# Convolution gates of three channel pairs as seven products of quarters, with weight sums made in DRAM

## The chip, the cores and the metric

The kernel runs on one core of a Trainium2 chip. The metric is the device time of one execution in microseconds (us), the median of several runs. The core has a matrix engine (PE, with its weight loads shown apart as PEld), a vector engine (DVE), a scalar engine (ACT), GpSimd (POOL) and a sync engine (SP), which here only issues transfers. Each has its own queue of instructions and waits for the others by semaphores.

## The reference

Two layers over 512 tokens of width D = 1024. Layer 0 mixes tokens with a forgetting attention, layer 1 with a short gated convolution. After each mixer come a squared-ReLU MLP (1024 to 4096 to 1024) and a gated per-layer embedding (PLE); every sub-layer stands between two RMS norms and is added to the residual. The change is in layer 1's mixer:

```python
def short_conv(h, w_in, conv_w, w_out):
    proj = h @ w_in                      # w_in: 1024 x 3072
    b_gate = proj[..., :D]
    c_gate = proj[..., D:2 * D]
    u = proj[..., 2 * D:]
    z = c_gate * u
    zc = causal_depthwise_conv(z, conv_w)   # 3 taps
    return (b_gate * zc) @ w_out

def sq_relu_mlp(h, w_up, w_down):
    return jnp.square(jax.nn.relu(h @ w_up)) @ w_down
```

Everything is float32.

## The kernel before

**One matmul is three.** PE works on float32 values rounded to its own format, fp32r. `mm3` (L224) splits each operand into a rounded part (hi) and the remainder (lo) and issues three matmuls: hi by hi (L226), hi by lo or lo by hi (L227, L228). `split` (L232) makes the parts: ACT rounds (L234), DVE subtracts (L235).

**Weights are streamed.** All weight tiles of the kernel stand in one list in the order of use. `fetch` (L117) brings the next, 256 KB as 128 rows of 512 values, into one of 14 raw buffers by a transfer on SP (L123); `prepare` (L137) splits it into the tiles `wh` and `wl`, eight tiles ahead of their use (`SOON`, L34). They live in a pool of 70 pages of 128x512. Results gather in 8 PSUM banks of 128x512.

**The MLP.** Hidden channels are worked in eight groups of 512 (`mlp`, L728). `up` makes a group's activations. `down` (L774) multiplies groups 0 to 6 by seven products of quarters in Winograd's form of Strassen's scheme: tokens by halves of the group on the one side, halves of the group by halves of the output on the other (PRODUCTS, L49; order of the products in STEPS, L53: 1, 2, 4, 5, 6, 7, 3). The weight side needs the sums T1 to T4, which `derive` (L125) makes on POOL from raw tiles; their lo parts, `wl<-T`, are also split on POOL. The activations' sums s are made on POOL as well (`quarters`, L757, sums at L760). `acc` banks gather the seven results over the groups.

**The convolution.** `conv` (L675) goes over four pairs of channel blocks, i0 = 0, 2, 4, 6; a block is 128 channels. `gates` (L690) makes c and u of a block, each by 8 k tiles x 3 = 24 matmuls, copies c to an SBUF page (ACT, L695) and multiplies (DVE, L696). `finish` (L700) makes b in the same way, applies the three taps (ACT L704, DVE L707), multiplies by b (L711) and splits the result for the output projection. Pair 0 is done in two halves of 256 tokens, so that it can begin before the last tokens of the layer before are ready; the other three pairs take 512 tokens at once. Its input `hT` is the normed and transposed residual, written as hi and lo by `pre_norm` (L288) in layer 0's PLE. Pairs read 12 weight tiles each (`wci`).

**Order.** A scheduler orders each engine's instructions by its own estimates of when each can run, from the order in which the program issues them; only few places set the order by hand. A pool's buffer is reused in program order.

Of the kernel before, what the change touches and what calls it, by code (L numbers as in the profile page):

```python
# [8 lines left out]
F32 = mybir.dt.float32  # L9
F32R = mybir.dt.float32r  # L10
AF = mybir.ActivationFunctionType
ALU = mybir.AluOpType
# [3 lines left out]
P = 128  # L16
D = 1024
S = 512
# [3 lines left out]
KT = D // P  # L22
# [30 lines left out]
STEPS = (1, 2, 4, 5, 6, 7, 3)  # L53


class Pair:


# [5 lines left out]


@with_exitstack
def trunk(ctx: ExitStack, tc, g4T, x, xT, pT, g, g0T, wv, wqk, bf, wo, wci, cw, wco, wup, wdn, wpp, wpg, out):
# [8 lines left out]
    dram = pool("dram", 1, space=DRAM)  # L76
# [40 lines left out]
    def fetch(upto):  # L117
        while len(fetched) < min(upto, len(loads)):
            n = len(fetched)
            raw = raws.tile([P, S], F32, tag="raw", name=f"raw{n}")  # L120
            fetched.append(raw)
            src = loads[n]
            nc.sync.dma_start(raw[:, : src.shape[-1]], src)  # L123

    def derive(l, gr):  # L125
        at = derived.pop((l, gr))
# [35 lines left out]
    def wide(*key, soon=SOON):  # L162

        prepare(where[key] + 1 + soon)
        return ready[key]

    def narrow(*key, k, c, soon=SOON):

        c += k % 2 * 256
        return wide(*key, k // 2, soon=soon).at(lambda u: u[:, c : c + P])  # L170

    for l in range(2):
        if l == 0:
            for c, (_, width) in enumerate(V_CHUNKS):
                for k in range(KT * width // 512 if width < 272 else KT):
                    plan(("v", c, k), wv[c][k])
            for i in range(KT):
                for j in range(4):
                    plan(("qk", i, j), wqk[i, j])
            for k in range(KT):  # L180
                for n in range(2):
                    plan(("o", n, k), wo[n, k])
        else:
            for i in range(0, KT, 2):
                for s, key in enumerate((("cu", i), ("b", i), ("cu", i + 1))):
                    for j in range(4):
                        plan((*key, j), wci[3 * (i // 2) + s, j])
# [100 lines left out]
    def pre_norm(t, xs, gB, hT, name):  # L288

        r = stats(t, xs, name)  # L290
        hs = [scaled(t, n, xs, r, gB, name) for n in range(2)]

        def turn():
            for n in range(2):
                keep(t, n, turned(t, n, hs[n], name), hT)

        put_off(t, turn)

# [373 lines left out]
            pass  # L672
        return oT[0], banks_o

    def conv(hT):  # L675
        taps = consts.tile([P, KT, 3], F32, tag="taps", name="taps")
        nc.sync.dma_start(taps, cw)
        ys = []

        def project(key, s, name, lo, hi):  # L680
            need(*range(lo // P, hi // P))
            ps = bank(name)
            for k in range(KT):
                mm3(
                    ps[:, : hi - lo], narrow(*key, k=k, c=s * P),
                    hT.at(lambda h: h[:, k, lo:hi]), k == 0, k == KT - 1,
                )
            return ps

        def gates(i, z, lo, hi):  # L690
            n = hi - lo
            c = project(("cu", i), 0, f"c{i}_{lo}", lo, hi)
            u = project(("cu", i), 1, f"u{i}_{lo}", lo, hi)
            cs = page(f"cs{i}_{lo}")
            nc.scalar.copy(cs[:, :n], c[:, :n])  # L695
            nc.vector.tensor_tensor(  # L696
                out=z[:, lo:hi], in0=u[:, :n], in1=cs[:, :n], op=ALU.mult
            )

        def finish(i, z, y, lo, hi):  # L700
            n = hi - lo
            b = project(("b", i - i % 2), i % 2, f"b{i}_{lo}", lo, hi)
            a = page(f"za{i}_{lo}")
            nc.scalar.mul(a[:, :n], z[:, lo:hi], taps[:, i, 2:3])  # L704
            for w in (1, 0):
                c = max(2 - w - lo, 0)
                nc.vector.scalar_tensor_tensor(  # L707
                    out=a[:, c:n], in0=z[:, lo + c + w - 2 : hi + w - 2],
                    scalar=taps[:, i, w : w + 1], in1=a[:, c:n], op0=ALU.mult, op1=ALU.add,
                )  # L710
            nc.vector.tensor_tensor(out=a[:, :n], in0=b[:, :n], in1=a[:, :n], op=ALU.mult)  # L711
            split(y.hi[:, lo:hi], y.lo[:, lo:hi], a[:, :n])

        for i0 in range(0, KT, 2):
# [12 lines left out]

    def mlp(l, hT, xs, then, late):  # L728
# [28 lines left out]
        def quarters(gr, f, q, s, A):  # L757

            L, R = slice(0, S // 2), slice(S // 2, S)
            sums = lambda out, a, b, op: nc.gpsimd.tensor_tensor(out=out, in0=a, in1=b, op=op)  # L760
# [56 lines left out]

        total, hs, gB = combine(), [], []
# [83 lines left out]
    hT = turned_x  # L902
# [4 lines left out]
    kind = "o"  # L907
    xs = [load_x("xb", t) for t in range(NB)]
    for l in range(2):
        if l == 1:  # L910
            lhs, kind, opened = conv(hT), "co", {}
        g1, g2 = gain(l, 1), gain(l, 2)
        hT = turned_x
        mixer_out(
# [28 lines left out]
        if l == 0:  # L943
            g0 = gain(1, 0)
            hT = turned_x
            then = lambda t: pre_norm(t, xs[t], g0, hT, "n0b")
# [11 lines left out]
def layout(x, p, norm_g, w_attn_in, b_forget, w_attn_out, w_conv_in, conv_w, w_conv_out,  # L958
# [26 lines left out]
    ci = np.stack([c[:, :, 0], u[:, :, 0], b[:, :, 0], b[:, :, 1], c[:, :, 1], u[:, :, 1]], axis=2)  # L985
    got["wci"] = tiles(ci.reshape(D, 3 * D), 2, 256)
# [26 lines left out]
```

## Time and profile before

| | |
|---|---|
| runs | 1230.38, 1230.71, 1231.73 us; median 1230.71 |
| the profiled execution | 1231.44 us |
| its span in the profile | 1229.7 us |
| PE busy | 1213.8 us, 99%, 5976 matmuls, granted clock 0.998 |
| DVE, ACT, POOL busy | 857.4, 673.5 and 642.2 us |
| transfers | 145.54 MB, mean 118 GB/s |

The trace shows one execution; start times count from the start of its span. In a row of groups the columns are line, engine, operation, out<-in, shapes, count, then busy us and mean ns of one, then idle time before and what ended it. In a row of the timeline they are start, length, engine, line, operation, out<-in, shapes and count of instructions taken together. Busy times of neighbouring matmuls overlap by some, so the pace of matmuls is read from windows or from starts.

### The profile page before, as it was taken

What the parts mean: (1) busy time and instruction counts of PE and PEld (TensorE: products, weight loads), DVE (VectorE), ACT (ScalarE), POOL (GpSimd) and SP (SyncE); (2) the same over time, 40 slices, a digit from 0 to 9 for tenths busy, and PEclk for the clock granted to TensorE, in tenths of its full rate; (3) what the DMA queues carried; (4) which work ended last, traced back from release to release, by engine and by line L of the source; (5) the groups of instructions that cost most, each with busy time, mean ns of one, the idle gap of its engine ahead of it and who ended that gap; (6) DMA issues with size and microseconds to landing.
All of it is one profiled execution on the core that took longest, in us unless ns stands there. A gap on an engine that the chain in (4) does not pass through costs nothing.

```text
span 1229.7 us, 17957 instructions
## 1 busy us (share of the span) xinstructions
PE 1213.8 (99%) x5976; PEld 1025.7 (83%) x5976; DVE 857.4 (70%) x1306; ACT 673.5 (55%) x1382; POOL 642.2 (52%) x650
## 2 busy tenths in 40 slices
PE   9999999999999999999999999999999999999997
PEld 8888887888888888888889888889888888888885
DVE  5668888585778766879757444556767787669952
ACT  6567888558634563456744322335756345645641
POOL 2058676057877877775310000027867878678220
PEclk9999999999999999999999999999999999999999
DMA  9564542623244223437323233432422443236401
GB/s 293 189 183 120 138 127 63 206 98 98 72 137 138 88 69 119 137 95 266 103 69 104 69 103 93 149 119 70 138 69 76 130 137 101 63 111 191 134 19 51
DMA packets 84173, 145.54 MB, mean 118 GB/s; under 512 B 10032, under 2 KB 17248, under 8 KB 84080
## 3 DMA queue, kind: packets, MB, share of 16 engines
q1 hardware_dynamic: 83648, 143.87, 38.0%
q8 instruction: 47, 0.77, 0.3%
q10 hardware_dynamic: 432, 0.53, 0.1%
q14 instruction: 46, 0.38, 0.1%
HBM read 137.99 MB, written 6.37 MB: 117 GB/s over the span
## 4 chain that ended last, share of the span: by engine, by line
PE 91%; DVE 3%; ACT 2%; DMA 2%; issue 1%; POOL 1%; SPq 0%; DVEq 0%; POOLq 0%; ACTq 0%
PE up L228 9%; PE up L226 9%; PE up L227 9%; PE dn L228 8%; PE dn L227 8%; PE dn L226 8%; PE pg L228 2%; PE pg L226 2%; PE pg L227 2%; PE qk L226 2%; PE qk L227 2%; PE qk L228 2%; PE v L227 1%; PE sc L495 1%; PE v L228 1%; PE v L226 1%
## 5 line engine op out<-in xcount | busy, mean ns | idle before, releaser
L235 DVE TENSOR_TENSOR wl<-raw,wh 128x512 fp32r<-128x512 f32 (+1 forms) x372 | 352.3, 993 | 24.6 <-ACT wh L234 16.7
L227 PE MATMUL up<-hTl,wh 128*128 128x512 f32 (+1 forms) x576 | 210.4, 366 | 0.5 <-DVE hTl L235 0.5
L228 PE MATMUL up<-hTh,wl 128*128 128x512 f32 (+1 forms) x576 | 209.7, 366 | 0.0
L226 PE MATMUL up<-hTh,wh 128*128 128x512 f32 (+1 forms) x576 | 209.6, 366 | 0.0
L234 ACT CAST wh<-raw 128x512 fp32r<-128x512 f32 (+1 forms) x372 | 202.9, 618 | 3.4 <-DMA raw<-in_wv 3.1
L235 POOL TENSOR_TENSOR wl<-T,wh 128x512 fp32r<-128x512 f32 x112 | 155.9, 1421 | 32.6 <-ACT wh L234 31.3
L746 ACT ACTIVATE r<-up 128x512 f32<-128x512 f32 (+1 forms) x72 | 39.3, 546 | 203.2 <-PE up L228 203.2
L792 DVE TENSOR_TENSOR acc<-dn,acc 128x512 f32<-128x512 f32 x168 | 107.9, 679 | 26.5 <-PE dn L228 26.5
L227 PEld LDWEIGHTS up<-hTl,wh 128*128 128x128 f32 x576 | 108.7, 189 | 18.2 <-DVE hTl L235 0.7
L228 PEld LDWEIGHTS up<-hTh,wl 128*128 128x128 f32 x576 | 108.7, 189 | 17.3
L226 PEld LDWEIGHTS up<-hTh,wh 128*128 128x128 f32 x576 | 108.4, 189 | 17.5
L135 POOL TENSOR_TENSOR T<-raw,raw 128x512 f32<-128x512 f32 x56 | 87.9, 1580 | 50.5 <-DMA raw<-in_wdn 36.9
L135 POOL TENSOR_TENSOR T<-raw,T 128x512 f32<-128x512 f32 x56 | 90.4, 1614 | 2.2
L256 POOL TENSOR_SCALAR cor_r_v<-cos,cos 128x1 f32<-128x1 f32 x4 | 1.8, 439 | 158.9 <-ACT junk L264 158.8
L234 ACT CAST wh<-T 128x512 fp32r<-128x512 f32 x112 | 61.4, 616 | 7.0 <-POOL T L135 7.0
L235 DVE TENSOR_TENSOR A12l<-q,A12h 128x512 fp32r<-128x512 f32 x28 | 24.5, 876 | 50.9 <-ACT A12h L234 50.9
L235 DVE TENSOR_TENSOR A11l<-q,A11h 128x256 fp32r<-128x256 f32 x28 | 25.4, 906 | 40.6 <-ACT A11h L234 40.6
L799 POOL TENSOR_TENSOR acc<-acc,acc 128x512 f32<-128x512 f32 x28 | 47.1, 1713 | 10.0 <-DVE acc L792 10.0
L226 PE MATMUL qk<-hTh,wh 128*128 128x512 f32 x128 | 51.0, 398 | 0.0
L226 PE MATMUL pg<-wh,hTh 128*128 128x512 f32 x128 | 50.5, 395 | 0.0
L228 PE MATMUL qk<-hTh,wl 128*128 128x512 f32 x128 | 50.5, 394 | 0.0
L227 PE MATMUL qk<-hTl,wh 128*128 128x512 f32 x128 | 50.2, 393 | 0.0
(246 smaller groups left out, 3160.4 us busy)
## 6 DMA issues: line engine op xcount, KB each, us to landing
raw<-in_wup SPq DMA_DIRECT2D x128, 256.0 KB, 2.9
raw<-in_wdn SPq DMA_DIRECT2D x128, 256.0 KB, 2.8
raw<-in_wci SPq DMA_DIRECT2D x48, 256.0 KB, 3.1
raw<-in_wqk SPq DMA_DIRECT2D x32, 256.0 KB, 5.9
raw<-in_wpg SPq DMA_DIRECT2D x32, 256.0 KB, 3.5
g<-in_g SPq DMA_DIRECT2D x18, 256.0 KB, 6.4
prl<-neg_c SPq DMA_DIRECT2D x16, 256.0 KB, 6.9
raw<-in_wo SPq DMA_DIRECT2D x16, 256.0 KB, 2.8
```

What stands on the lines that cost most here:

```text
L135: nc.gpsimd.tensor_tensor(out=B[name, p], in0=B[a, p], in1=B[b, p], op=ALU.subtract)
L226: nc.tensor.matmul(ps, a.hi, b.hi, start=start, stop=False)
L227: nc.tensor.matmul(ps, a.hi, b.lo, start=False, stop=False)
L228: nc.tensor.matmul(ps, a.lo, b.hi, start=False, stop=stop)
L234: nc.scalar.copy(hi, src)
L235: eng.tensor_tensor(out=lo, in0=src, in1=hi.bitcast(F32), op=ALU.subtract)
L256: nc.gpsimd.tensor_scalar(out=v, in0=parts[0], scalar1=parts[1], scalar2=EPS, op0=ALU.add, op1=ALU.add)
L495: nc.tensor.matmul(ps[:, :nm], at[:, b * P : n], to[:, :nm], start=s == 0, stop=s == 1)
L746: nc.scalar.activation(r[:, :n], ps[:, :n], AF.Relu)
L792: nc.vector.tensor_tensor(out=a, in0=banks[s], in1=a, op=ALU.add)
L799: nc.gpsimd.tensor_tensor(out=a, in0=a, in1=acc[i, s][:, :S], op=ALU.add)
```

## The change

For the pairs i0 = 2, 4, 6 the c and u projections are one product of a 512x1024 by a 1024x512 matrix (tokens by k, and k by the four blocks c and u of both blocks of the pair), cut into quarters: token halves by k halves, and k halves by two channel blocks. `sevenths` makes the seven products, in the order 1, 6, 7, 5, 2, 4, 3 (PARTS), each two column halves x 4 k tiles x 3 matmuls of 256 columns. DVE combines them (U, V, W, c11, c12, c21, c22, all 128x512; ACT copies the first product to `cp`), and z comes from four half products. b stays as it was, and pair 0 too.

The token side needs four sums (s1 to s4). For them eight fp32 copies of the transposed tokens (`plain`) are made by ACT out of PSUM when `hT` is written, and `token_sums`, called once within pair 0, makes and splits the sums.

The weight side needs t1 to t4 for each of the three pairs. They are made in DRAM while layer 0's MLP runs: `sum_weights(gr)` is called after `up` of group gr. In group 0 SP copies a quarter into each of t1 and t3 (six transfers of 512 KB), in group 1 GpSimd adds another quarter with accumulating transfers (six), in group 2 t1 is copied to t2 (three), in group 3 b22 is added (three), in group 4 t2 is copied to t4 and in group 5 b21 is added. Copies are issued behind the group's last raw fetch, accumulates behind its last quarter sum. Each pair then streams 14 tiles for the products and 4 for b in place of 12.

```diff
+SUMS_W = {"t1": ("b11", "b12"), "t3": ("b12", "b22"), "t2": ("t1", "b22"), "t4": ("t2", "b21")}
+SUM_STEPS = (
+    (("t1", "copy"), ("t3", "copy")), (("t1", "add"), ("t3", "add")), (("t2", "copy"),),
+    (("t2", "add"),), (("t4", "copy"),), (("t4", "add"),), (),
+)
+PARTS = (
+    (1, "a11", "b11"), (6, "s2", "t2"), (7, "s3", "t3"), (5, "s1", "t1"),
+    (2, "a12", "b21"), (4, "a22", "t4"), (3, "s4", "b22"),
+)
...
-            nc.sync.dma_start(raw[:, : src.shape[-1]], src)
+            behind["copy"] = nc.sync.dma_start(raw[:, : src.shape[-1]], src)
...
+    def sum_weights(step):
+
+        of = lambda n, i: sums_w[n][i] if n in sums_w else wcs[QUARTERS.index(n), i]
+        for name, kind in SUM_STEPS[step]:
+            a, b = SUMS_W[name]
+            with tc.issue_after(behind[kind].ins):
+                for i in range(3):
+                    if kind == "copy":
+                        nc.sync.dma_start(sums_w[name][i], of(a, i))
+                    else:
+                        nc.gpsimd.dma_start(
+                            sums_w[name][i], of(b, i), accum_op=ALU.add, max_dma_last_dim=2048
+                        )
...
+        def token_sums():
...
+                for name, a, b, op in (
+                    ("s3", p[0, 0], p[1, 0], ALU.subtract), ("s1", p[1, 1], p[1, 0], ALU.subtract),
+                    ("s2", p[0, 0], "s1", ALU.add), ("s4", "s2", p[0, 1], ALU.subtract),
+                ):
...
+                    nc.vector.tensor_tensor(out=t[:, :S], in0=a, in1=b, op=op)
...
+        def sevenths(i0):
...
+            for i, a, b in PARTS:
+                ps = bank(f"sq{i}_{i0}")
+                for s in range(2):
+                    w = wide("sq", i0, s, b)
+                    for k in range(4):
+                        mm3(
+                            ps[:, s * half : (s + 1) * half],
+                            w.at(lambda u: u[:, k * P : (k + 1) * P]), part_of(a, k), k == 0, k == 3,
+                        )
+                if i == 1:
+                    cp = page(f"cp_{i0}")
+                    nc.scalar.copy(cp[:, :S], ps)
+                    got["cp"] = cp[:, :S]
+                elif i == 6:
+                    tt("U", ps, "cp")
+                elif i == 7:
+                    tt("V", "U", ps)
+                elif i == 5:
+                    tt("W", "U", ps)
+                    tt("c22", "V", ps)
+                elif i == 2:
+                    tt("c11", "cp", ps, ALU.add)
+                elif i == 4:
+                    tt("c21", ps, "V")
+                else:
+                    tt("c12", "W", ps)
...
-            for lo, hi in ((0, 256), (256, 512)) if i0 == 0 else ((0, 512),):
+            if i0:
+                for (e, h), m in sevenths(i0).items():
+                    nc.vector.tensor_tensor(
+                        out=zs[e][:, (L, R)[h]], in0=m[:, L], in1=m[:, R], op=ALU.mult
+                    )
+                for i in range(2):
+                    finish(i0 + i, zs[i], both[i], 0, S)
+                ys += both
+                continue
+            for lo, hi in (0, 256), (256, 512):
                 gates(i0, zs[0], lo, hi)
+                if lo:
+                    token_sums()
...
             up(gr, done)
+            if l == 0:
+                sum_weights(gr)
             down(gr, A)
```

The scheduler also orders the engines anew. On POOL, in group 1 of layer 0's MLP, before (s120 and s340 are the group's last quarter sums, wl106 to wl109 the lo parts of the tiles of T2 and T3):

```order
L760 TENSOR_TENSOR s340_1_2_4415<-q0_1_2_4239 128x256
L760 TENSOR_TENSOR s120_1_3_4449<-q0_1_2_4239,q0_1_3_4240 128x256
L760 TENSOR_TENSOR s120_1_3_4449<-s120_1_3_4449,q0_1_2_4239 128x256
L760 TENSOR_TENSOR s340_1_2_4415<-q0_1_3_4240,s120_1_3_4449 128x256
L235 TENSOR_TENSOR wl106_4464<-T2_0_1_0_4262,wh106_4463 128x512
L235 TENSOR_TENSOR wl107_4474<-T2_0_1_1_4270,wh107_4473 128x512
L235 TENSOR_TENSOR wl108_4488<-T3_0_1_0_4260,wh108_4487 128x512
L235 TENSOR_TENSOR wl109_4498<-T3_0_1_1_4268,wh109_4497 128x512
```

And after (wst1 and wst3 are t1 and t3 in DRAM, in_wcs the quarters of the convolution's weights):

```order
L890 TENSOR_TENSOR s340_1_2_4425<-q0_1_2_4249 128x256
L890 TENSOR_TENSOR s120_1_3_4459<-q0_1_2_4249,q0_1_3_4250 128x256
L890 TENSOR_TENSOR s120_1_3_4459<-s120_1_3_4459,q0_1_2_4249 128x256
L890 TENSOR_TENSOR s340_1_2_4425<-q0_1_3_4250,s120_1_3_4459 128x256
L194 DMA wst1_83<-in_wcs 256x512 x3
L194 DMA wst3_84<-in_wcs 256x512 x3
L272 TENSOR_TENSOR wl106_4480<-T2_0_1_0_4272,wh106_4479 128x512
L272 TENSOR_TENSOR wl107_4490<-T2_0_1_1_4280,wh107_4489 128x512
L272 TENSOR_TENSOR wl108_4504<-T3_0_1_0_4270,wh108_4503 128x512
L272 TENSOR_TENSOR wl109_4514<-T3_0_1_1_4278,wh109_4513 128x512
```

The accumulating transfers stand between the last quarter sum and the first of the splits, six of them in group 1; in groups 3 and 5 three stand at the same place.

On PE, at the end of the same group's `down`, before (dn0_1_60 is the bank of layer 0, group 1, product 6, output rows 0; wh106 and wl106 are the parts of T2's first tile):

```order
L226 MATMUL dn0_1_60_4561<-wh106_4463,S1h0_1_1_4359 128x512
L226 MATMUL dn0_1_61_4562<-wh106_4463,S1h0_1_1_4359 128x512
L227 MATMUL dn0_1_60_4561<-wl106_4464,S1h0_1_1_4359 128x512
L228 MATMUL dn0_1_60_4561<-wh106_4463,S1l0_1_1_4360 128x512
L227 MATMUL dn0_1_61_4562<-wl106_4464,S1h0_1_1_4359 128x512
L228 MATMUL dn0_1_61_4562<-wh106_4463,S1l0_1_1_4360 128x512
L226 MATMUL dn0_1_60_4561<-wh107_4473,S1h0_1_3_4453 128x512
L226 MATMUL dn0_1_61_4562<-wh107_4473,S1h0_1_3_4453 128x512
L226 MATMUL dn0_1_70_4589<-wh108_4487,S3h0_1_1_4363 128x512
L226 MATMUL dn0_1_71_4590<-wh108_4487,S3h0_1_1_4363 128x512
```

And after, from the same row on (up0_2_0_0 is the first bank of the next group's `up`):

```order
L263 MATMUL dn0_1_60_4577<-wh106_4479,S1h0_1_1_4369 128x512
L263 MATMUL dn0_1_61_4578<-wh106_4479,S1h0_1_1_4369 128x512
L263 MATMUL dn0_1_70_4605<-wh108_4503,S3h0_1_1_4373 128x512
L263 MATMUL dn0_1_71_4606<-wh108_4503,S3h0_1_1_4373 128x512
L263 MATMUL dn0_1_30_4633<-wh110_4527,S3h0_1_1_4373 128x512
L263 MATMUL dn0_1_31_4634<-wh110_4527,S3h0_1_1_4373 128x512
L263 MATMUL up0_2_0_0_4665<-hTh_87,wh112_4551 128x512
L264 MATMUL up0_2_0_0_4665<-hTl_88,wh112_4551 128x512
L263 MATMUL up0_2_1_0_4747<-hTh_87,wh112_4551 128x512
L264 MATMUL up0_2_1_0_4747<-hTl_88,wh112_4551 128x512
L264 MATMUL dn0_1_30_4633<-wl110_4528,S3h0_1_1_4373 128x512
```

The first read of wl106 comes in the second piece of after, further on:

```order
L263 MATMUL up0_2_0_0_4665<-hTh_87,wh113_4563 128x512
L264 MATMUL up0_2_0_0_4665<-hTl_88,wh113_4563 128x512
L265 MATMUL up0_2_1_0_4747<-hTh_87,wl112_4552 128x512
L263 MATMUL up0_2_1_0_4747<-hTh_87,wh112_4551 128x512
L264 MATMUL dn0_1_60_4577<-wl106_4480,S1h0_1_1_4369 128x512
L265 MATMUL dn0_1_60_4577<-wh106_4479,S1l0_1_1_4370 128x512
L264 MATMUL dn0_1_61_4578<-wl106_4480,S1h0_1_1_4369 128x512
```

Before, the first read of wl106 is the 51st matmul of the group's `down`; now it is the 77th, since product 3 and the first of the next `up` stand ahead of it. In groups 3 and 5 it is the 53rd.

More of the change, by code (lines that the diff above doesn't have):

```diff
@@ L165, in wide @@
         return ready[key]
+    behind = {}
+    sums_w = {n: dram.tile([3, P, 2 * S], F32, tag=f"ws{n}", name=f"ws{n}") for n in SUMS_W}
+    def sum_weights(step):
[10 more added lines that the diff above has]
+                        )
     def narrow(*key, k, c, soon=SOON):
@@ L673, in attention, with conv @@
         return oT[0], banks_o
-    def conv(hT):
+    def conv(hT, plain):
         taps = consts.tile([P, KT, 3], F32, tag="taps", name="taps")
@@ L712, in finish @@
             split(y.hi[:, lo:hi], y.lo[:, lo:hi], a[:, :n])
+        half = S // 2
+        L, R = slice(0, half), slice(half, S)
+        A = {
+            name: hT.at(lambda h: h[:, k0 : k0 + 4, c])
+            for name, k0, c in (("a11", 0, L), ("a12", 4, L), ("a22", 4, R))
+        }
+        def token_sums():
+            kept_at = {}
+            for j in range(2):
+                p = {(c, n): plain[2 * c + j, n][:, :S] for c in range(2) for n in range(2)}
+                for name, a, b, op in (
+                    ("s3", p[0, 0], p[1, 0], ALU.subtract), ("s1", p[1, 1], p[1, 0], ALU.subtract),
+                    ("s2", p[0, 0], "s1", ALU.add), ("s4", "s2", p[0, 1], ALU.subtract),
+                ):
+                    t = page(f"{name}_{j}")
+                    a, b = (kept_at[u, j] if isinstance(u, str) else u for u in (a, b))
+                    kept_at[name, j] = t[:, :S]
+                    nc.vector.tensor_tensor(out=t[:, :S], in0=a, in1=b, op=op)
+            four = lambda u: u.rearrange("p (k c) -> p k c", k=4)
+            two = lambda u: u[:, :S].rearrange("p (k c) -> p k c", k=2)
+            for name in ("s2", "s3", "s1", "s4"):
+                A[name] = [
+                    Pair(page(f"{name}h{d}", F32R), page(f"{name}l{d}", F32R)).at(two)
+                    for d in range(2)
+                ]
+                for d in range(2):
+                    for j in range(2):
+                        at = slice(j * P, (j + 1) * P)
+                        split(
+                            A[name][d].hi[:, :, at], A[name][d].lo[:, :, at],
+                            four(kept_at[name, j])[:, 2 * d : 2 * d + 2, :],
+                        )
@@ new lines, in part_of, with tt @@
+        def part_of(name, k):
+            if name in ("a11", "a12", "a22"):
+                return A[name].at(lambda h: h[:, k, :])
+            return A[name][k // 2].at(lambda h: h[:, k % 2, :])
+        def sevenths(i0):
+            got = {}
+            def tt(out, a, b, op=ALU.subtract):
+                t = page(f"{out}_{i0}")
+                a, b = (got[u] if isinstance(u, str) else u for u in (a, b))
+                nc.vector.tensor_tensor(out=t[:, :S], in0=a, in1=b, op=op)
+                got[out] = t[:, :S]
+            for i, a, b in PARTS:
+                ps = bank(f"sq{i}_{i0}")
+                for s in range(2):
+                    w = wide("sq", i0, s, b)
[21 more added lines that the diff above has]
+                    tt("c12", "W", ps)
+            return {(e, h): got[f"c{h + 1}{e + 1}"] for e in range(2) for h in range(2)}
@@ L759, in quarters, with sums @@
             L, R = slice(0, S // 2), slice(S // 2, S)
-            sums = lambda out, a, b, op: nc.gpsimd.tensor_tensor(out=out, in0=a, in1=b, op=op)
+            def sums(out, a, b, op):
+                behind["add"] = nc.gpsimd.tensor_tensor(out=out, in0=a, in1=b, op=op)
             if f % 2 == 0:
@@ L910, in trunk @@
         if l == 1:
-            lhs, kind, opened = conv(hT), "co", {}
+            lhs, kind, opened = conv(hT, plain), "co", {}
         g1, g2 = gain(l, 1), gain(l, 2)
@@ L945, in trunk, with copied @@
             hT = turned_x
-            then = lambda t: pre_norm(t, xs[t], g0, hT, "n0b")
+            plain = {}
+            def copied(t, n, ps):
+                plain[t, n] = page(f"hp{t}_{n}")
+                nc.scalar.copy(plain[t, n][:, :S], ps)
+            then = lambda t: pre_norm(t, xs[t], g0, hT, "n0b", copied)
         else:
```

31 lines of the change are left out of this document (22 added, 9 removed).

## Prediction

> **What bounds the kernel now.** I read the page's busy times first, then its chain that ended last, then windows of the stages that the change touches.
>
> ```profile
> span 1229.7 us, 17957 instructions
> PE 1213.8 (99%) x5976; PEld 1025.7 (83%) x5976; DVE 857.4 (70%) x1306; ACT 673.5 (55%) x1382; POOL 642.2 (52%) x650
> PE 91%; DVE 3%; ACT 2%; DMA 2%; issue 1%; POOL 1%; SPq 0%; DVEq 0%; POOLq 0%; ACTq 0%
> ```
>
> PE is busy for 99% of the span and is 91% of the chain, so the time is PE's column count plus whatever PE waits for. The change can gain only by feeding PE less, and lose only by making it wait. Next, the conv stage: columns are PE, PEld, DVE, ACT, POOL busy, then PE's granted clock, DMA share and GB/s. The first window is channel pair 0, the second the three pairs that change (with the edges of their neighbours).
>
> ```profile
> 650.64:685.00 34.36, 34.36 (x289) 34.35 (x288) 20.79 (x39) 14.49 (x33) 1.72 (x4) 1.00 0.30 93
> 686.93:784.88 97.95, 97.95 (x434) 81.16 (x433) 41.54 (x65) 28.47 (x51) 0.00 (x0) 1.00 0.36 108
> ```
>
> PE has no gap in either, at clock 1.00; DVE works 41.54 of 97.95 us and ACT 28.47. There is room on the helpers, none on PE.
>
> **The saving on PE.** The same windows, of the c banks alone (columns PE, PEld, ACT, clock, DMA, GB/s):
>
> ```profile
> 650.64:653.51 2.87, 2.87 (x24) 2.83 (x23) 0.00 (x0) 1.00 0.00 0
> 719.60:725.04 5.44, 5.44 (x24) 4.32 (x23) 0.00 (x0) 1.00 0.28 76
> ```
>
> Twenty-four matmuls of 256 columns take 2.87 us, 0.1196 each; 24 of 512 take 5.44 us, 0.2267 each. Halving the columns does not quite halve the time: 2 x 0.1196 is 0.0125 more than 0.2267, and this tax is what the change pays. Per pair it removes 4 x 24 = 96 matmuls of 512 columns, 21.76 us, and adds 7 products x 2 column halves x 4 k tiles x 3 = 168 of 256, 20.09 us. That is 1.67 us per pair, **5.0 us** for three. The b projections, taps and outputs stay. The 0.1196 was measured where a weight load (PEld 2.83 of 2.87 us) stands before each matmul, as it does in the seven products, so it carries over.
>
> **The helpers beside the seven products.** Rows of DVE and then ACT, from 675 to 780 us:
>
> ```profile
> L235 DVE TENSOR_TENSOR wl<-raw,wh 128x512 fp32r<-128x512 f32 x36 | 22.6, 685 | 0.0
> L696 DVE TENSOR_TENSOR z<-u,cs 128x512 f32<-128x512 f32 x6 | 4.1, 692 | 41.0 <-PE u L228 41.0
> L707 DVE SCALAR_TENSOR_TENSOR za<-z,taps,za 128x511 f32<-128x511 f32 x5 | 3.7, 748 | 1.6 <-ACT za L704 1.6
> L696 DVE TENSOR_TENSOR z<-u,cs 128x256 f32<-128x256 f32 x2 | 0.8, 424 | 5.8 <-PE u L228 5.8
> L234 ACT CAST wh<-raw 128x512 fp32r<-128x512 f32 x36 | 19.6, 617 | 0.0
> L695 ACT COPY cs<-c 128x512 f32<-128x512 f32 x6 | 3.5, 587 | 14.2 <-PE c L228 14.2
> L704 ACT ACTIVATE za<-z,taps 128x512 f32<-128x512 f32 x5 | 3.6, 724 | 22.0 <-DVE z L696 22.0
> L234 ACT CAST yh<-za 128x256 fp32r<-128x256 f32 x2 | 0.8, 408 | 2.8 <-DVE za L711 2.8
> ```
>
> Per pair, DVE now splits 18 weight tiles instead of 12 (18 x 0.685 = 12.3), makes seven combinations (7 x 0.692 = 4.8) and four half products (4 x 0.424 = 1.7), and keeps the taps (4 x 0.75), two products with b and two splits (4 x 0.692): 24.6 us. PE has 20.1 us of products and two b projections of 5.44, 31.0 in all. ACT has 18 x 0.617 + 0.587 + 2 x 0.724 + 2 x 0.617 = 14.4 us. Both fit. In the products alone DVE has 14 splits, the combinations and the half products, 16.1 of 20.1 us: tight, not over. The token sums (eight of 128x512, 16 splits of half that size: 8 x 0.692 + 16 x 0.424 = 12.3 us of DVE; with eight plain copies 16 x 0.408 + 8 x 0.587 = 11.2 of ACT) fall near pair 0, where the window above leaves DVE 34.36 - 20.79 = 13.6 us and ACT 19.9. That just fits, so I cost it at nothing; if the cover is gone, DVE's pending c, u and b results hold PSUM banks and PE stops for some microseconds (rival C).
>
> Raw tiles: 14 of 256 KB in 20.1 us are 183 GB/s. The trace shows more with PE unbroken (window 540 to 580, last column), and such a tile lands in 3.1 us:
>
> ```profile
> 540.00:580.00 40.00, 40.00 (x178) 33.13 (x178) 39.49 (x45) 21.08 (x39) 23.43 (x15) 1.00 0.77 257
> raw<-in_wci SPq DMA_DIRECT2D x48, 256.0 KB, 3.1
> ```
>
> **The accumulating transfers on POOL.** GpSimd issues six after the last quarter sum of group 1 of layer 0's MLP, three after that of group 3, three of group 5, each 512 KB. They stand ahead of the wl splits of T2 and T3 on POOL, and PE needs those. POOL's and PE's timelines around groups 1, 3 and 5 (start, length):
>
> ```profile
> 328.22 0.74 POOL L760 TENSOR_TENSOR s<-q,s 128x256 f32<-128x256 f32 x1
> 330.22 5.97 POOL L235 TENSOR_TENSOR wl<-T,wh 128x512 fp32r<-128x512 f32 x4 [1.25 <-ACT wh L234]
> 342.09 1.29 POOL L135 TENSOR_TENSOR T<-raw,raw 128x512 f32<-128x512 f32 x1 [5.90 <-DMA raw<-in_wdn]
> 324.26 0.39 PE L226 MATMUL dn<-wh,A11h 128*128 128x512 f32 x1
> 409.37 0.74 POOL L760 TENSOR_TENSOR s<-q,s 128x256 f32<-128x256 f32 x1
> 411.37 6.12 POOL L235 TENSOR_TENSOR wl<-T,wh 128x512 fp32r<-128x512 f32 x4 [1.25 <-ACT wh L234]
> 405.86 0.39 PE L226 MATMUL dn<-wh,A11h 128*128 128x512 f32 x1
> 492.97 6.12 POOL L235 TENSOR_TENSOR wl<-T,wh 128x512 fp32r<-128x512 f32 x4 [1.25 <-ACT wh L234]
> ```
>
> In the changed order of PE, 76 matmuls stand between group 1's first product and the first read of T2's low half, so that is due at 324.26 + 76 x 0.2267 = 341.5. POOL is free at 328.96 and each split takes 1.49: with d us per transfer the half is ready at 328.96 + 6d + 1.49, in time while d is at most 1.84. In groups 3 and 5 there are 52 matmuls (due 417.65) and three transfers: 410.11 + 3d + 1.53, in time while d is at most 2.0 (group 5's splits stand the same 1.25 us idle behind its sum). Above that PE loses 6(d - 1.84) + 2 x 3(d - 2.0) = 12d - 23.0 us. The derivation of T behind them has 5.90 us of idle to give.
>
> The trace has no GpSimd transfer. The nearest rows:
>
> ```profile
> 342.25 0.33 SPq L123 DMA_DIRECT2D raw<-in_wup  x1
> L135 POOL TENSOR_TENSOR T<-raw,raw 128x512 f32<-128x512 f32 x56 | 87.9, 1580 | 50.5 <-DMA raw<-in_wdn 36.9
> 331.56 1.76 DVE L235 TENSOR_TENSOR S1l<-s,S1h 128x512 fp32r<-128x512 f32 x1
> ```
>
> From below: SP issues 128 rows in 0.33 us, so 256 rows in 0.66. From above: two POOL passes over 256 KB each, 3.2 us. It issues and does not touch the data, so it is nearer the first; I take d = 1 and no stall. The Trainium skill ("DMA: Bandwidth & Descriptors", Latency and other measured facts) puts the first byte of a GpSimd-issued transfer at about 1 us; by it the sum is the same, and no run here shows it.
>
> **The copies on SP.** The first six stand behind raw tiles issued near 240 us and cost issue time only. The t2 copies wait for group 1's accumulates, and the raw tiles of group 3's up projection are queued behind them. Those are issued from 342.25 (row above); PE first reads one here:
>
> ```profile
> 384.10 0.39 PE L226 MATMUL up<-hTh,wh 128*128 128x512 f32 x1
> ```
>
> Six accumulates are 3.15 MB: at 257 GB/s and each byte once, 12.2 us; read twice and written once, 36.7. Started between 329 and 335, they land between 341 and 372. Then three copies (1.57 MB, 6.1 us, or 12.2 if counted twice), a tile of 2.9 to 3.1 us and its split of 1.3: ready between 352 and 389 against 384.1. I take nothing; the far end is rival D. Moving t1 to t4 early costs nothing else: they are read 300 us later.
>
> **Sum.** The profiled execution, 1231.44 (span 1229.7), less 5.0 is 1226.4. It stands 0.73 above the runs' median of 1230.71, which gives **1225.7**. The measurement can tell about 0.2% from no change: faster is under 1228.25, slower over 1233.2.
>
> **Rivals.**
>
> *A, slower: the transfers hold POOL.* If d is the far end, 3.2 us, PE loses 12 x 3.2 - 23.0 = 15.4 us: 1230.71 + 10.4 = 1241. It eats the gain from d = 2.33 on and is measurably slower from 2.54. For it: six of them stand in one queue ahead of a split that PE is due to read 12.5 us after POOL comes free. Against: 3.2 is a price for arithmetic, and these only issue. 0.09.
>
> *B, no change: GpSimd is locked out while DVE works.* DVE's S1l split took 1.76 us beside POOL at 331.56, against 0.685 in its row L235, so the two share something. Should each issue wait out one such instruction, d = 0.66 + 1.76 = 2.42, PE loses 6.0 and the time is 1231.7. The Trainium skill ("SBUF — State Buffer", two separate sides) states such a rule: while DVE holds the shared ports, GpSimd can't write its descriptors; but the same page (Who interferes with whom) infers that a two-input operation, which DVE's are here, holds only the read side. The 1.76 shows contention with POOL arithmetic, not with an issue. 0.05.
>
> *C: helpers late at the conv stage's entry or in the products.* DVE's 16.1 of 20.1 us and the token sums' 12.3 in 13.6 leave little; 2 to 4 us lost give 1227.7 to 1229.7. Against: no PE gap there now. 0.10, half of it faster.
>
> *D: accumulates land late*, SP holds group 3's raw tiles, PE waits up to 389 - 384.1 = 5 us in group 3, and less for the smaller later ones: 1227.7 to 1230.7. 0.10, a fifth of it faster.
>
> *E, more gain: the tax per matmul is smaller in a long stream.* With none, 256 columns take half of 0.2267, 0.1133: 168 x 0.1133 = 19.04, 2.72 less than 21.76 per pair, 8.2 in all and 1222.5; with a quarter of it, 1223.4. Against: the 0.1196 is the mean of 24 in a row with no gap. The Trainium skill ("TensorE: Matmul & The Clock Gate", Back-to-back issue gap) gives the gap of an isolated matmul as N/2.4 + 2.5 ns, by which the saving would be 7.1 us and the time 1223.6; the trace lies 10.4 ns above that at 256 columns. 0.04.
>
> That the change does not do what it says is excluded: PE has 6174 matmuls in its order against 5958, the 3 x 72 more.
>
> **How the numbers follow.** The forecast has 0.62. Faster: 0.62 + E 0.04 + half of C 0.05 + 0.02 of D = 0.73. Same: B 0.05 + C 0.05 + D 0.08 = 0.18. Slower: A 0.09. The range goes from 1224.0 to 1231.0; it leaves out A, B and E, 0.18, and holds C, D and the forecast, whose own range is 1224.7 to 1227.0.
>
> **What would show it.** Right: sq products of 24 matmuls in 2.87 us with no PE gap from 650 to 780, a pair in 31.0 us, GpSimd's transfers of 1 us or less between the last s and the first wl<-T of groups 1, 3 and 5, and no wait on PE before dn<-wl there. A: PE idle before dn<-wl, released by POOL. B: the same with transfers of 2.4 us that end where DVE's instructions end. C: PE released by DVE or ACT between 650 and 780. D: DMA ending the wait before the up projection near 384. A saving per pair other than 1.67 makes the pace wrong.

## The result, and the profile after

| | median, us | runs |
|---|---|---|
| before | 1231.22 | 1230.38 to 1231.73, 5 runs |
| after | 1244.21 | 1240.48 to 1245.63, 5 runs |

The ratio is 1.0103 (95% interval 1.0091 to 1.0115): the change makes the kernel 1% slower, where 0.4% faster was forecast. The profiled execution of after took 1244.68 us with a span of 1242.8, against 1231.44 and 1229.7.

The span and the busy times of after's page:

```profile
span 1242.8 us, 18637 instructions
PE 1219.9 (98%) x6192; PEld 1037.0 (83%) x6192; DVE 903.0 (73%) x1375; ACT 690.8 (56%) x1421; POOL 649.6 (52%) x662
```

PE's busy time went up by 6 us although its columns went down, and its share fell to 98%: it now waits, and it is slower at places. Where, the starts of the first product of each group's `down` in layer 0's MLP tell (PE's timeline of both kernels; the difference in the last row):

| group | 1 | 2 | 3 | 4 | 5 | 6 |
|---|---|---|---|---|---|---|
| before, us | 324.26 | 365.06 | 405.86 | 446.66 | 487.46 | 528.25 |
| after, us | 324.13 | 374.04 | 414.83 | 460.12 | 500.92 | 545.58 |
| later by | -0.13 | 8.98 | 8.97 | 13.46 | 13.46 | 17.33 |

Groups 1, 3 and 5, those with accumulating transfers, lose 9.11, 4.49 and 3.87 us, 17.5 together; 2 and 4 lose nothing. The convolution does what was forecast. Its three pairs as a window of after, then the first pair's products alone (same columns as the windows of before; the second row's are PE, PEld, DVE, ACT, clock, DMA, GB/s):

```profile
704.29:797.47 93.18, 93.18 (x650) 87.51 (x649) 70.32 (x121) 39.09 (x72) 0.00 (x0) 1.00 0.52 162
704.29:724.45 20.16, 20.16 (x168) 20.11 (x168) 4.05 (x6) 0.58 (x1) 1.00 0.52 160
```

93.18 us against 97.95 is 4.77 less, PE has no gap, and 168 matmuls of 256 columns take 20.16 us. From pair 0's first matmul to the first pair of three it is 36.29 us in both kernels (650.64 to 686.93, and 668.00 to 704.29): the token sums cost nothing.

What happens in group 1. First PE's list of waits in after, then its timeline, then DVE's and POOL's:

```profile
PE dn L265 <- DVE S1l L272: 4.1, 1, 4.1
PE dn L263 <- DVE acc L923: 3.6, 2, 1.9
```

```profile
334.33 0.39 PE L264 MATMUL dn<-wl,S1h 128*128 128x512 f32 x1
338.83 1.22 PE L265 MATMUL dn<-wh,S1l 128*128 128x512 f32 x2 [4.11 <-DVE S1l L272]
```

```profile
330.23 1.29 DVE L923 TENSOR_TENSOR acc<-dn,acc 128x512 f32<-128x512 f32 x2 [2.77 <-PE dn L265]
331.44 7.34 DVE L272 TENSOR_TENSOR S1l<-s,S1h 128x512 fp32r<-128x512 f32 x1
338.70 1.75 DVE L272 TENSOR_TENSOR S3l<-s,S3h 128x512 fp32r<-128x512 f32 x1
```

```profile
328.82 5.67 POOL L194 DMA_DIRECT2D wst<-in_wcs  x6
332.49 7.40 POOL L272 TENSOR_TENSOR wl<-T,wh 128x512 fp32r<-128x512 f32 x4
```

The records of the six transfers last 5.67 us together, 0.94 each. The T splits behind them begin 3.67 us after the first transfer (0.61 for each of the six), while the last records still run to 334.49. They are done at 339.89, ahead of the 341.5 at which PE would have read them. POOL is not late. But DVE's subtraction that makes S1l, 1.76 us before, takes 7.34, and PE stands for it. The accumulations `acc`, which read one input from PSUM and one from SBUF, go on at their 0.65 each while the transfers are issued. In groups 3 and 5 it is S3l that takes long. PE does not wait for S3l itself there but for an `acc` that stands behind it in DVE's queue (the second row of PE's waits above). Group 3 on DVE, then on POOL:

```profile
420.02 0.69 DVE L923 TENSOR_TENSOR acc<-dn,acc 128x512 f32<-128x512 f32 x1 [0.37 <-PE dn L265]
420.63 6.68 DVE L272 TENSOR_TENSOR S3l<-s,S3h 128x512 fp32r<-128x512 f32 x1
```

```profile
419.03 2.68 POOL L194 DMA_DIRECT2D wst<-in_wcs  x3
420.75 6.00 POOL L272 TENSOR_TENSOR wl<-T,wh 128x512 fp32r<-128x512 f32 x4
```

S3l comes free at 427.31, half a microsecond after the last of POOL's four splits (426.75). Group 5 on POOL, then on DVE:

```profile
505.12 2.69 POOL L194 DMA_DIRECT2D wst<-in_wcs  x3
506.84 6.01 POOL L272 TENSOR_TENSOR wl<-T,wh 128x512 fp32r<-128x512 f32 x4
```

```profile
506.03 0.69 DVE L272 TENSOR_TENSOR S1l<-s,S1h 128x512 fp32r<-128x512 f32 x1
507.23 6.17 DVE L272 TENSOR_TENSOR S3l<-s,S3h 128x512 fp32r<-128x512 f32 x1
```

Here S1l, with both inputs in SBUF, ran at 0.69 us in the midst of the issuing; S3l, which began after POOL's splits had, took 6.17. Then the clock (windows of after, groups 1, 3 and 5; the column behind POOL's):

```profile
337.11:347.34 10.23, 8.21 (x17) 5.35 (x18) 10.23 (x14) 2.18 (x4) 2.79 (x2) 0.50 1.12 215
429.27:432.68 3.41, 3.41 (x9) 2.64 (x9) 3.41 (x7) 0.00 (x0) 0.00 (x0) 0.50 0.28 79
514.60:518.01 3.41, 3.38 (x9) 2.68 (x9) 3.41 (x7) 0.61 (x2) 0.00 (x0) 0.50 0.45 107
```

In group 1 the granted clock falls to half at 337.11, while PE still stands, and stays there until 347.34; for the last 8.5 us of it PE works, and does the work of half that time. So some 4.5 us of standing and some 4.3 of half clock make nearly all of the 9.1 us. In groups 3 and 5 waits of 1.87 and 1.74 us are followed by 3.41 us at half clock each, which costs another 1.7; together that is most of the 4.49 and 3.87.

### The profile page after: what moved, and what is told of

It is laid out like the page before. It is cut to its first block, busy times and chain, and to the rows that moved or that the text cites. A ratio compares the mean times of both kernels' runs of the same rounds, so it can differ in the third digit from the quotient of the medians.

```text
span 1242.8 us, 18637 instructions
## 1 busy us (share of the span) xinstructions
PE 1219.9 (98%) x6192; PEld 1037.0 (83%) x6192; DVE 903.0 (73%) x1375; ACT 690.8 (56%) x1421; POOL 649.6 (52%) x662
## 3 DMA queue, kind: packets, MB, share of 16 engines
q0 software_dynamic: 3264, 6.29, 2.9%
## 4 chain that ended last, share of the span: by engine, by line
PE 89%; DVE 3%; ACT 3%; DMA 2%; issue 1%; POOL 1%; DVEq 0%; POOLq 0%; ACTq 0%; SPq 0%
PE up L263 9%; PE up L264 9%; PE up L265 9%; PE dn L263 8%; PE dn L265 8%; PE dn L264 8%; PE pg L265 2%; PE pg L263 2%; PE pg L264 2%; PE qk L263 2%; PE qk L264 2%; PE qk L265 2%; PE sq L265 2%; PE sq L264 2%; PE sq L263 2%
## 5 line engine op out<-in xcount | busy, mean ns | idle before, releaser
L272 DVE TENSOR_TENSOR wl<-raw,wh 128x512 fp32r<-128x512 f32 (+1 forms) x390 | 359.8, 968 | 25.4 <-ACT wh L271 21.2
L271 ACT CAST wh<-raw 128x512 fp32r<-128x512 f32 (+1 forms) x390 | 213.1, 620 | 12.1 <-DVE S3l L272 3.7
```

What stands on the lines that cost most here:

```text
L271: nc.scalar.copy(hi, src)
L272: eng.tensor_tensor(out=lo, in0=src, in1=hi.bitcast(F32), op=ALU.subtract)
```

## The experiments

Three theories stood after reading the two traces. **Theory 1**: while GpSimd issues transfers, DVE instructions with two inputs in SBUF are held; PE waits for S1l and S3l and then runs at half clock. **Theory 2**: the transfers' traffic delays raw tiles. **Theory 3**: the copies, token sums or products cost the time. Each group of runs had its own runs of before beside it (medians 1231.23, 1230.64 and 1230.77 us).

**Without the accumulates.**

```diff
         for name, kind in SUM_STEPS[step]:
+            if kind == "add":
+                continue
```

> The twelve accumulating transfers are left out (t1 to t4 stay plain copies of one quarter, so c and u of three pairs are not the reference's); copies, token sums and seven products stay. Theory 1 (GpSimd's issuing holds DVE's two-input instructions, and PE waits for them at half clock): the 17.4 us lost in layer 0's MLP are gone and the conv stage's 4.8 stay, 1226.4. Theory 2 (the transfers' traffic delays the raw tiles): also about 1226. Theory 3 (the copies, the token sums or the products themselves cost it): 1240 or more.

Measured: 1225.95 us, ratio 0.9954 (0.9939 to 0.9968). Theory 3 falls: everything but the twelve transfers is worth 5.3 us, and the whole loss hangs on them. (Without them the scheduler also put PE's order back to that of before. The order isn't what makes the loss: the two orders part at the 51st matmul of group 1's `down`, and the wait of 4.11 us stands ahead of the 47th.)

**Plain transfers by GpSimd.**

```diff
-                        nc.gpsimd.dma_start(
-                            sums_w[name][i], of(b, i), accum_op=ALU.add, max_dma_last_dim=2048
-                        )
+                        nc.gpsimd.dma_start(sums_w[name][i], of(b, i), max_dma_last_dim=2048)
```

> The twelve transfers stay on GpSimd at the same places and with the same rows, but copy instead of accumulating (sums are then only the second quarter, not the reference's). Theory 1: nothing changes for DVE, since it is the issue that holds it: 1244, S1l of group 1 near 7.3 us. Theory 2: a copy reads one operand less, a third of the traffic gone: 1236 to 1240. If accumulating itself is what costs: 1226.

Measured: 1235.11 us, ratio 1.0033 (1.0022 to 1.0044), between all the guesses. Group 1 on POOL, then on DVE:

```profile
329.00 3.57 POOL L194 DMA_DIRECT2D wst<-in_wcs  x6
332.58 5.48 POOL L270 TENSOR_TENSOR wl<-T,wh 128x512 fp32r<-128x512 f32 x4
```

```profile
331.63 0.68 DVE L270 TENSOR_TENSOR S1l<-s,S1h 128x512 fp32r<-128x512 f32 x1
332.23 4.70 DVE L270 TENSOR_TENSOR S3l<-s,S3h 128x512 fp32r<-128x512 f32 x1
```

This does not fit Theory 1 as put, and neither did group 5 of the changed kernel: S1l ran in 0.68 us in the midst of the issuing. S3l, 0.6 us later, met the beginning of POOL's splits and took 4.70. The six records last 3.57 us together instead of 5.67, though POOL's splits begin as soon after the first of them (3.58 us, 3.67 before), and groups 1, 3 and 5 lose 4.48, 1.92 and 1.29 us (starts of the products as above). Accumulating isn't needed for the loss, only makes it larger.

**The same bytes by SP.**

```diff
-            with tc.issue_after(behind[kind].ins):
+            with tc.issue_after(behind["copy"].ins):
...
-                        nc.gpsimd.dma_start(
-                            sums_w[name][i], of(b, i), accum_op=ALU.add, max_dma_last_dim=2048
-                        )
+                        nc.sync.dma_start(sums_w[name][i], of(b, i), max_dma_last_dim=2048)
```

> The twelve transfers are plain copies issued by SP behind the group's last raw tile, with the same 256 rows (sums are then only the second quarter, not the reference's). Theory 1: GpSimd issues nothing, DVE is free: 1226.4. Theory 2: the bytes now stand right among the raw tiles: 1235 or more, with DMA as the releaser of ACT and POOL in groups 1 to 6.

Measured: 1226.28 us, ratio 0.9958 (0.9943 to 0.9973). A window of it, columns as before:

```profile
340.00:360.00 20.00, 20.00 (x90) 16.55 (x89) 19.86 (x22) 4.57 (x8) 16.16 (x12) 1.00 0.83 288
```

288 GB/s on the queues and PE has no gap. A plain copy reads one operand less than an accumulate, so the traffic isn't quite the same, but nothing here speaks for Theory 2.

**The transfers behind the T splits.** `sum_weights` is called behind `down`, and the marker is the group's last wl split on POOL.

```diff
-                split(hi[:, :w], lo[:, :w], raw[:, :w], eng)
+                last = split(hi[:, :w], lo[:, :w], raw[:, :w], eng)
+                if eng is nc.gpsimd:
+                    behind["add"] = last
...
             up(gr, done)
+            down(gr, A)
             if l == 0:
                 sum_weights(gr)
-            down(gr, A)
```

> The accumulating transfers go behind the group's last wl split of T on POOL, where POOL was idle (5.9 us in group 1). Theory 1: S1l and S3l run undisturbed, but in group 1 DVE's wl splits of the next raw tiles stand from 338.5 to about 342, and the first of them is read at 341.0: 1 to 2 us of waiting with as much lost to the clock in group 1, less in 3 and 5: 1228 to 1232. A rival, that PE waits for POOL's own splits of T2 and T3: those are no longer behind the transfers, 1226.4.

Measured: 1226.59 us, ratio 0.9964 (0.9951 to 0.9976), with all of the change's work. POOL, then DVE in group 1:

```profile
335.78 5.67 POOL L196 DMA_DIRECT2D wst<-in_wcs  x6
346.20 1.29 POOL L149 TENSOR_TENSOR T<-raw,raw 128x512 f32<-128x512 f32 x1 [4.75 <-DVE acc L925]
```

```profile
338.19 2.48 DVE L274 TENSOR_TENSOR wl<-raw,wh 128x512 fp32r<-128x512 f32 x4
```

Theory 1's price was too high, and the row says why: four wl splits, two SBUF inputs each, run at 0.62 us while GpSimd issues six accumulating transfers. **Issuing alone held nothing here.** Nothing that reads SBUF stands close behind the transfers in group 1 (POOL's next work starts at 346.20). In group 5 a T subtraction does, from 501.10, and four wl splits beside it take 4.04 us in place of 2.48; PE doesn't wait for them. So the theory was amended: what holds DVE is a POOL instruction that reads SBUF and has begun while part of GpSimd is still issuing.

**Longer rows.**

```diff
-                            sums_w[name][i], of(b, i), accum_op=ALU.add, max_dma_last_dim=2048
+                            sums_w[name][i], of(b, i), accum_op=ALU.add, max_dma_last_dim=8192
```

> Each accumulating transfer has 64 rows of 8 KB instead of 256 of 2 KB; places and bytes stay, and the output is the reference's. Theory 1, with the hold lasting as long as the rows are written out: the hold falls to about a quarter, S1l from 7.3 to 2 to 3 us, PE waits hardly or not at all: 1227 to 1231. If the hold is per transfer or lasts until POOL's splits are done whatever the rows: 1240 to 1244. Theory 2 (traffic): 1244, the bytes are the same.

Measured: 1240.54 us, ratio 1.0076 (1.0059 to 1.0093). POOL, then DVE in group 1:

```profile
329.16 5.04 POOL L194 DMA_DIRECT2D wst<-in_wcs  x6
```

```profile
331.79 6.71 DVE L272 TENSOR_TENSOR S1l<-s,S1h 128x512 fp32r<-128x512 f32 x1
```

A quarter of the rows take the six records from 5.67 to 5.04 us together and S1l from 7.34 to 6.71. The hold doesn't go by rows.

**The transfers between derivations.** Three at a time behind the fourth T subtraction of groups 1, 2, 3 and 5.

```diff
...
+            if l == 0 and p == 0 and gr in ADDS:
+                add_weights(ADDS[gr], op)
...
```

> The accumulating transfers go three at a time behind the fourth subtraction that derives T on POOL, in groups 1 (t1), 2 (t3), 3 (t2) and 5 (t4), where DVE's next two-input work is wl splits that PE reads 10 us later. Theory 1: DVE is held as long as before, but nothing that PE needs soon: 1226.4 to 1228. A rival, that any twelve such transfers cost POOL and DVE time that PE is short of: 1235 or more.

Measured: 1227.56 us, ratio 0.9975 (0.9966 to 0.9984). POOL, then DVE:

```profile
306.66 2.96 POOL L198 DMA_DIRECT2D wst<-in_wcs  x3
308.64 3.53 POOL L147 TENSOR_TENSOR T<-raw,raw 128x512 f32<-128x512 f32 x2
```

```profile
307.18 6.79 DVE L277 TENSOR_TENSOR wl<-raw,wh 128x512 fp32r<-128x512 f32 x2
```

Here a POOL instruction that reads SBUF follows at once, and the hold is there: two splits take 6.79 us, and beside POOL one takes about 1.78. But PE reads these tiles much later, so it costs little. The first of the two took 1.77 us although POOL's next read is recorded 1.46 us after its start, and S1l in group 1 of the changed kernel would alone have been through at 332.1, ahead of the first split's record at 332.49. So either part of GpSimd reads ahead of the record, or the end of issuing can hold DVE too; no run parts the two.

**S1 late, with no transfer at all.** Into the kernel before:

```diff
+            if l == 0 and gr == 1 and f == 3:
+                for i in range(9):
+                    nc.vector.tensor_tensor(
+                        out=s12[:, :S], in0=s12[:, :S], in1=s12[:, :S], op=ALU.max
+                    )
             halves(gr, f, ("S1", "S2"), s12, A)
```

> The kernel before with nothing of the change; in group 1 of layer 0's MLP DVE takes the maximum of S1's source with itself nine times ahead of its split (the values stay), which makes S1 about 6 us late. Theory 1, that lateness of S1l alone is enough: PE waits some 3 to 4.5 us and then runs at half clock for 6 to 9 us, together 6 to 9 us: 1237 to 1240. If the half clock came from the transfers: 1234 to 1236, the wait alone.

Measured: 1240.11 us, ratio 1.0078 (1.0063 to 1.0094). PE, and a window behind it:

```profile
340.47 0.79 PE L226 MATMUL dn<-wh,S1h 128*128 128x512 f32 x1 [7.01 <-ACT S1h L234]
```

```profile
340.00:345.00 5.00, 4.53 (x14) 3.65 (x15) 3.28 (x5) 5.00 (x10) 3.46 (x3) 0.65 0.01 2
```

Lateness of S1 alone stops PE and lowers its clock, without a transfer. The shares came out otherwise: the wait was longer (7.0 us, since the nine steps held ACT's cast of S1 too) and the half clock shorter (336.63 to 343.46, 3.8 us of it within the wait).

**The place of the change, with a wait behind the transfers.** This tells the amended theory from the first.

```diff
+            with tc.issue_after(last.ins):
+                mark = nc.gpsimd.memset(x, 0.0)
+            nc.scalar.copy(y, x)
+            with tc.issue_after(mark.ins):
+                behind["sync"] = nc.gpsimd.tensor_scalar(
+                    out=z, in0=y, scalar1=1.0, scalar2=1.0, op0=ALU.add, op1=ALU.add
+                )
```

(The first split of T2 is issued behind that last instruction.)

> The transfers stay where the change has them, ahead of POOL's wl splits of T2 and T3, but behind them GpSimd writes one column, ACT copies it, and GpSimd reads the copy before it goes on: the splits begin only when all of GpSimd is done with issuing. Theory 1 as first put (issuing holds DVE): S1l and S3l still meet the transfers, 7 and 6 us, 1240 or more. Theory 1 amended after the run with the transfers behind the splits (what holds DVE is a POOL instruction that reads SBUF and has begun while part of GpSimd is still issuing): S1l and S3l take 1.8 us at most, the splits are 1 to 2 us later and in time, 1226.5 to 1229.

Measured: 1226.79 us, ratio 0.9968 (0.9956 to 0.9979). POOL in group 1, then DVE (the last row stands beside the splits):

```profile
328.68 5.66 POOL L201 DMA_DIRECT2D wst<-in_wcs  x6
334.77 0.23 POOL L210 TENSOR_SCALAR sync<-sync 128x1 f32<-128x1 f32 x1 [0.32 <-ACT sync L208]
334.97 1.27 POOL L176 TENSOR_TENSOR wl<-T,wh 128x512 fp32r<-128x512 f32 x1
```

```profile
330.90 0.68 DVE L288 TENSOR_TENSOR S1l<-s,S1h 128x512 fp32r<-128x512 f32 x1
331.50 0.69 DVE L288 TENSOR_TENSOR S3l<-s,S3h 128x512 fp32r<-128x512 f32 x1
336.80 2.97 DVE L288 TENSOR_TENSOR wl<-raw,wh 128x512 fp32r<-128x512 f32 x2 [0.47 <-ACT wh L287]
```

Same transfers, same place, and S1l and S3l take 0.69 us. S3l starts 2.8 us after the first transfer here, as S1l did in the changed kernel (2.6), so it met the same moment of issuing. Beside the splits that follow the wait, DVE's two-input splits take 1.5 us each, no longer than S1l and S3l beside POOL before the change. In group 3 an instruction that only writes follows the transfers at once, and S3l beside it is not held (POOL, then DVE):

```profile
412.21 1.12 POOL L207 MEMSET sync<- 128x1 f32 x1
```

```profile
412.50 0.68 DVE L288 TENSOR_TENSOR S3l<-s,S3h 128x512 fp32r<-128x512 f32 x1
```

So the first form of Theory 1 falls, and Theory 2 with it, since the traffic is the same. Of the amended one these runs show that POOL work which reads SBUF must follow the transfers without a wait: with a wait, or with a small write behind them, nothing was held. That part of GpSimd must still be issuing is not shown: behind plain transfers the splits begin at 332.58, where the transfers' records end, and S3l was held all the same. The splits begin 2.5 us later than in the changed kernel and are still in time. Group 1 loses 1.05 us in place of 9.11: PE waits 0.67 us for ACT, whose casts of T stand behind its copy of the column.

**Waits of five lengths.** Into the kernel before, S1 delayed by gr + 1 steps in groups 1 to 5.

```diff
+            if l == 0 and 1 <= gr <= 5 and f == 3:
+                for i in range(gr + 1):
+                    nc.vector.tensor_tensor(
+                        out=s12[:, :S], in0=s12[:, :S], in1=s12[:, :S], op=ALU.max
+                    )
```

> The kernel before with nothing of the change; S1's source is delayed on DVE by 2, 3, 4, 5 and 6 instructions in groups 1 to 5 of layer 0's MLP (the values stay), which gives PE five waits between 0 and about 4 us. If the clock falls only after a wait of more than 3 us, the shorter ones cost what they last; if any wait of over 1.5 us halves it, as groups 3 and 5 of the changed kernel suggest (1.87 and 1.74 us waited, 4.5 and 3.9 us lost), each costs about twice what it lasts. Together 5 to 15 us, 1236 to 1246.

Measured: 1252.03 us, ratio 1.0172 (1.0154 to 1.0191; two runs). PE's waits in groups 3 and 4, and the windows with them:

```profile
421.51 0.69 PE L226 MATMUL dn<-wh,S1h 128*128 128x512 f32 x1 [3.50 <-ACT S1h L234]
...
467.79 0.50 PE L226 MATMUL dn<-wh,S1h 128*128 128x512 f32 x1 [3.58 <-ACT S1h L234]
```

```profile
418.24:421.65 3.41, 0.14 (x1) 0.14 (x2) 2.67 (x6) 0.81 (x2) 0.00 (x0) 1.00 0.00 0
421.65:425.06 3.41, 3.41 (x9) 2.64 (x10) 2.25 (x4) 3.41 (x8) 2.49 (x2) 0.50 0.00 0
...
462.61:466.03 3.42, 1.60 (x8) 0.98 (x6) 3.31 (x6) 0.00 (x0) 0.00 (x0) 1.00 0.00 0
466.03:469.44 3.41, 1.65 (x7) 1.38 (x8) 2.46 (x5) 2.33 (x5) 0.59 (x1) 1.00 0.00 0
469.44:472.85 3.41, 3.06 (x14) 2.21 (x13) 3.08 (x4) 3.41 (x8) 3.41 (x3) 1.00 0.00 0
```

Neither guess holds, and the time lies above the expected 1236 to 1246: groups 1 to 5 lose 1.40, 2.41, 5.41, 4.54 and 6.29 us. A wait of 3.50 us lowered the clock and one of 3.58 did not, while 1.87 and 1.74 did in the changed kernel. By length alone it can't be said which wait costs double.

The traces say more. Ahead of the last microseconds of a run, every stretch of half clock in them lasts 3.41 us or two or three times that, and the stretches of one trace lie on one grid of 3.41 us; the windows here are cut along it. The wait of 3.50 us fell almost whole into one interval (PE busy 0.14 us), and the next one ran at half clock. The one of 3.58 us fell half into each of two (1.60 and 1.65 busy), and none did. The waits of 1.87 and 1.74 us left PE busy for 1.32 and 1.67 us of theirs. So where a wait falls on the grid counts beside its length; the busy time at which the clock falls can't be read from these runs (1.67 was too little in one, 1.60 enough in the other).

**The better version again.** The kernel with the transfers behind the splits, in more rounds.

> The version with the transfers behind the splits once more with more rounds, for its interval against the kernel before: 1226 to 1227, ratio 0.996.

Measured: 1226.29 us, ratio 0.9962 (0.9948 to 0.9976). It beats both kernels: 4.5 us below before.

## Why the prediction was wrong, point by point

- **The saving on PE** was right: 4.77 us of 5.0, the pace 0.120 us per matmul of 256 columns, no gap in the stage.
- **The helpers beside the products**, the token sums and the raw tiles were rightly costed at nothing (rival C did not come).
- **The price of a transfer on POOL**, d = 1, was right or a little high (0.94 by the records, 0.61 by the start of the splits behind them), and so was that the T splits come in time (339.89 against 341.5). Rival A's mechanism did not occur, though its time, 1241, is near the measured one.
- **The step that failed** is the one from there to "no stall". The sum followed POOL's queue and asked who waits for POOL; it didn't ask what runs on DVE while POOL goes straight from the transfers to its splits. S1l and S3l run there, and PE reads S1l 3 us after it starts. S1l took 7.34 us in group 1, S3l 6.68 and 6.17 in groups 3 and 5, in the place of 1.8 or less, and PE stood 4.11, 1.87 and 1.74 us for them or for the `acc` behind them.
- **Rival B** had the shared resource and the row that shows it (S1l at 1.76 beside POOL against 0.685 alone), but the direction wrong: GpSimd was not held by DVE, DVE was held by GpSimd. The Trainium skill ("SBUF — State Buffer", Who interferes with whom) says that a DVE instruction with two SBUF inputs contends with a GpSimd instruction that reads SBUF. The runs agree: before the change S1l and S3l took 1.76 and 1.78 us beside POOL's splits, and two `acc` behind them, with one input in PSUM, 1.28 us together from 334.95 on, beside the last of these splits, which ended at 336.19.
- **That a short wait costs its length** was taken silently in 12d - 23.0. In after, waits of about 8 us in all lost 17.5.
- **The range** left out A and B as rare. Nothing in the profile of before priced a GpSimd transfer beside DVE; that unknown deserved more than 14 in 100.
- **SP's copies and the traffic** (rival D) cost nothing: with DVE's hold gone, the kernel takes 1226.29 us, within 0.6 us of the forecast's sum.

What stays open is why the hold lasts over several POOL instructions. Before the change DVE got in between two of POOL's splits (1.76 and 1.78 us); behind transfers S3l of group 3 lasted until all four were done. The Trainium skill ("GPSIMD Engine Reference", Instruction dispatch) says that consecutive GpSimd instructions are no barrier between its cores. If the cores that issue lag behind the others, some core is reading at every moment until the row of instructions ends; the run with the wait fits that, since waiting brings them together. The lengths of POOL's records fit it in part. Group 1's four splits in the kernel before, in the changed kernel and behind plain transfers:

```profile
L235 POOL TENSOR_TENSOR wl<-T,wh 128x512 fp32r<-128x512 f32 x4 | 6.0, 1520 | 1.3 <-ACT wh L234 1.3
L272 POOL TENSOR_TENSOR wl<-T,wh 128x512 fp32r<-128x512 f32 x4 | 7.4, 3350 | 0.0
L270 POOL TENSOR_TENSOR wl<-T,wh 128x512 fp32r<-128x512 f32 x4 | 5.5, 1403 | 0.0
```

In the changed kernel a split lasts 3.35 us on average, and four take 7.4: they overlap. Behind plain transfers they don't, and S3l was held for 4.70 us all the same. So a lag may make the hold longer, but it isn't shown to be its cause. No run shows the single cores.

## What to carry to other kernels

Moving work to an idle queue has a price for its neighbours too: look at what the other engines run at that moment and when their results are read, not only at that queue's own slack. GpSimd transfers cost about 1 us at most in this kernel where POOL had a wait behind them, and cost 17.5 us where POOL's next SBUF read followed at once beside urgent two-input work on DVE. Where PE is 99% busy, a wait of 2 us can cost 4.

## Not expected of the hardware

- The records of six accumulating transfers of 512 KB on POOL lasted 5.67 us together with 256 rows and 5.04 with 64, of six plain ones 3.57; POOL's next instruction began 3.67, 3.34 and 3.58 us after the first.
- DVE's 128x512 subtraction with two SBUF inputs took 0.69 us alone, 1.78 beside POOL's splits, and 4.7 to 7.3 beside splits that follow transfers at once.
- PE's clock was halved for 3.41 us after waits of 1.74, 1.87 and 3.50 us and for 10.2 us around one of 4.11, and not at all after one of 3.58 us that fell across two intervals of the 3.41 us grid.
